# Branch A of an encoder layer: transposes and value products taken for four tiles at a time, blocks turned in place, and a last output piece on another queue

## The chip, the cores and the metric

The kernel runs on one core of one Trainium2 chip. The metric is the device time of one execution in microseconds (us). Engines are named as in the profile: PE is TensorE's matmul side, PEld its weight loads, DVE VectorE, ACT ScalarE, POOL GpSimd, SP SyncE, which here only issues transfers.

## The reference

One encoder layer over two inputs (1024 sample rows, 256 prompt rows; width 1024). Branch A is attention with a window of 128 on either side, 8 query heads on 2 key/value heads, a bias by relative position and a sink logit for each head. Branch B is a dilated attention of three head groups. Both are gated, merged and projected; a squared-ReLU MLP and a last norm follow.

```python
s = jnp.einsum('bnqgrd,bnkgd->bngrqk', qb, kb).astype(jnp.float32) * (dh ** -0.5)
logits = jnp.where(valid[None, :, None, None], s + bias, NEG_INF)
m = jnp.max(logits, axis=-1)
m = jnp.maximum(m, sink_r)                      # branch A only
p = jnp.exp(logits - m[..., None])
denom = jnp.sum(p, axis=-1) + jnp.exp(sink_r - m)
o = jnp.einsum('bngrqk,bnkgd->bnqgrd', p.astype(vb.dtype), vb)
o = o / denom
...
merged = gates[:, :, 0] * (o_a @ w_branch_a) + gates[:, :, 1] * (o_b @ w_branch_b)
x = x + merged @ w_out
return x + jnp.square(jax.nn.relu(rmsnorm(x) @ w_up)) @ w_down     # then a last rmsnorm
```

## The kernel before

The whole program is in stages that PE works through one after the other. Input projections and branch B come first (up to 554 us of the profiled execution), then branch A (554 to 675 us), the gate and branch projections (to 756 us), w_out, and the MLP to the end. Within branch A the order of every engine's instructions is the order in which the code is written (`manual_schedule`).

**Branch A's loop.** There are 1280 rows in ten tiles of 128 (t 0 to 7 sample, 8 and 9 prompt) and four units (u 0 to 3) of two heads each, so 40 steps in `order`; the loop takes two of them per iteration, j = 0, 2, 4, ... A tile sees two or three blocks of 128 keys: blocks for t = 0 to 9 are 2, 3, 3, 3, 3, 3, 3, 2, 2, 2. With two heads a pair of tiles (t even, t+1) has 10, 12, 12, 10 and 8 blocks to turn in the five pairs of a unit.

- `scores(u, t)`: PE multiplies queries and keys into a bank `sc` for each head (L1214, L1215); DVE adds the bias and takes the row maximum in one instruction (L1216) into the tile `s`; a small DVE instruction makes the exponent's bias `nm_a` (L1220).
- `exponential(u, t, h)`: ACT, in place on `s` (L1226), with the row sum.
- `transposes(u, t)`: PE turns every block of a pair into banks of four blocks (L1240), bank tags `pt`, `pt`, `mm`; each bank is copied out to a tile `pt` in SBUF of its own, by ACT, DVE, ACT (`moved`, L282 and L284).
- `values_of(u, t)`: PE multiplies the turned blocks with the values into the one bank `pv` (L1256), with a 128x64 array for each head; DVE copies the result out (L1259), SP stores it to `scr_o`.
- `logits()`, called `fill`: the last gate columns. One `next(fill)` gives PE four matmuls of 512 columns or eight of 256 (L193, bank `mm`, written `mm` in the rows).
- `merge()`, called `merges`: branch B's merge, mostly POOL work with small steps on DVE and ACT in the same in-order queues.

PSUM banks: `bufs={"mm": 3, "sc": 2, "pt": 2, "pv": 1}` (L138), so there are two `pt` banks. In iteration j the code calls `values_of` of pair j-6, `transposes` of pair j-4, `scores` of j, one step of `fill`, the exponentials of j, `scores` of j+1, another step of `fill`, and the exponentials of j+1. At j = 40 `sums_a` closes the row sums, and the load of the sigmoid table and the gates follow. `end` (L1942 and on) makes the last output rows: SP sends both left quarters of the row (L1966), ACT the third quarter and POOL the last one (L1967).

Of the kernel before, what the change touches and what calls it, by code (L numbers as in the profile page):

```python
# [15 lines left out]
P = 128  # L16
# [6 lines left out]
HD = 64  # L23
# [75 lines left out]
def encoder_kernel(  # L99
# [1091 lines left out]
    if True:  # L1191
# [13 lines left out]

        def scores(u, t):
            st, bias = units[u]
            lo, W, c0 = tiles[t]
            s = a3("s", n=4)
            m = small.tile([P, 2], F32, name="m", tag="m")  # L1210
            for h in range(2):
# [5 lines left out]
                    s[:, h, :W], ps[:, :W], bias[:, h, c0 : c0 + W], 1.0, -3.0e38,  # L1217
# [4 lines left out]
            live[u, t] = s  # L1222

        def exponential(u, t, h):
            W, s = tiles[t][1], live[u, t]
            nc.scalar.activation(s[:, h, :W], s[:, h, :W], AF.Exp, bias=nm_a[:, 2 * u + h : 2 * u + h + 1, t],  # L1226
                                 accum_out=l_a[:, 2 * u + h : 2 * u + h + 1, t])

        def transposes(u, t):

            pt = a3("pt", (P, 12, P), 1)
            jobs, at = [], []
            for i in range(2):
                at.append(len(jobs))
                jobs += [(live[u, t + i], b, h) for b in range(tiles[t + i][1] // P) for h in range(2)]
            for i, tag, eng in ((0, "pt", nc.scalar), (4, "pt", nc.vector), (8, "mm", nc.scalar)):
                if i < len(jobs):
                    ps, e = bank(tag, "pt"), min(len(jobs), i + 4)
                    for k, (s, b, h) in enumerate(jobs[i:e]):
                        nc.tensor.transpose(ps[:, P * k : P * k + P], s[:, h, P * b : P * b + P], ident)  # L1240
                    moved(eng, pt[:, i:e, :], ps[:, : P * (e - i)].rearrange("p (i q) -> p i q", q=P))
            for i in range(2):
                live[u, t + i] = pt, at[i]

        def values_of(u, t):

            pv = bank("pv")
            for i in range(2):
                lo, W, _ = tiles[t + i]
                pt, at = live.pop((u, t + i))  # L1250
                v, rest = units[u][0]["v"]
                for b in range(W // P):
                    k = lo + b
                    src = v[:, k, HALVES[u // 2]] if k < 8 else rest[:, k - 8, HALVES[u // 2]]
                    for h in range(2):
# [170 lines left out]
    if True:  # L1426
# [101 lines left out]
        for j in range(0, n + 4, 2):  # L1528
# [629 lines left out]
```

## Time and profile before

| what | value |
|---|---|
| median of three runs | 1660.57 us (1660.44 to 1661.66) |
| the profiled execution | 1661.59 us |
| its span in the trace | 1659.8 us |
| PE busy | 1650.8 us, 99% of the span |
| DVE, ACT, POOL busy | 57%, 43%, 31% |
| granted TensorE clock | 1.00 in every slice |

The page gives each engine's busy time, the span in 40 slices, the DMA queues, the chain that ended last and the costliest groups. In the trace a timeline row reads: start, length, engine, line, operation, output tile <- inputs, shape, count, and in brackets the idle time ahead of it with what ended it. Matmul ends are modelled, so starts are the safer numbers. A piece of the chain reads: start, length, engine, tile and line, count.

### The profile page before, as it was taken

To read this page: it belongs to the slowest core of one execution; us is meant where nothing else is said; L and a number is where in the kernel's file an instruction comes from. 1 tells how busy PE (TensorE), PEld (TensorE's weight loads), DVE (VectorE), ACT (ScalarE), POOL (GpSimd) and SP (SyncE) were. 2 spreads that over 40 slices of the span, in tenths; PEclk is the share of its full clock that TensorE was granted. 3 is DMA by queue.
4 is the path that set the end of the run, shared out by engine and by line. 5 is a ranking of instruction groups with operands and counts; after the bars stand their busy time and mean duration, and the time that the engine had idled before them with its cause. 6 is when DMAs were issued, how large, how long until landed. Compare 5 with 4: busy or idle time off the path is not lost.

```text
span 1659.8 us, 25051 instructions
## 1 busy us (share of the span) xinstructions
PE 1650.8 (99%) x9383; PEld 1404.7 (85%) x9383; DVE 952.5 (57%) x1540; ACT 712.5 (43%) x1478; POOL 516.5 (31%) x397
## 2 busy tenths in 40 slices
PE   9999999999999999999999999999999999999998
PEld 7898888888888888888888888888888888888887
DVE  6732333435555477776478454454456675866665
ACT  6232323325565466653276333333334333333435
POOL 1332222130221525200101555555554250514240
PEclk9999999999999999999999999999999999999999
DMA  7424332655666786955022444344357934733343
GB/s 255 149 70 136 106 110 75 171 145 172 189 201 178 242 245 185 314 192 204 28 87 73 150 148 150 110 145 152 111 172 246 354 119 146 241 102 108 121 121 127
DMA packets 215489, 263.58 MB, mean 159 GB/s; under 512 B 21688, under 2 KB 143816, under 8 KB 215368
## 3 DMA queue, kind: packets, MB, share of 16 engines
q1 hardware_dynamic: 207320, 242.62, 45.8%
q0 software_dynamic: 7712, 18.96, 4.1%
q8 instruction: 74, 1.21, 0.3%
q14 instruction: 47, 0.39, 0.1%
q10 hardware_dynamic: 336, 0.40, 0.1%
HBM read 176.24 MB, written 89.87 MB: 160 GB/s over the span
## 4 chain that ended last, share of the span: by engine, by line
PE 90%; issue 4%; DVE 2%; DMA 2%; ACT 1%; POOL 1%; SPq 0%; POOLq 0%; DVEq 0%; ACTq 0%
PE x L365 20%; PE dn L365 18%; PE mm L193 11%; PE z L365 10%; PE v L863 6%; PE y L365 5%; PE mm L365 5%; PE sc L365 3%; PE pv L365 3%; PE pv L1256 2%; PE pt L1240 2%; PE pt L626 1%; PE sc L590 1%; PE pv L643 1%; PE tr L356 1%
## 5 line engine op out<-in xcount | busy, mean ns | idle before, releaser
L365 PE MATMUL dn<-dhi,ulo 128*128 128x512 f32 x448 | 174.3, 389 | 0.0
L365 PE MATMUL dn<-dlo,uhi 128*128 128x512 f32 x448 | 174.3, 389 | 0.0
L365 PE MATMUL dn<-dhi,uhi 128*128 128x512 f32 x448 | 174.3, 389 | 0.0
L365 PE MATMUL x<-chi,wlo 128*128 128x512 f32 x436 | 171.3, 393 | 0.0
L365 PE MATMUL x<-clo,whi 128*128 128x512 f32 x436 | 170.2, 390 | 0.0
L365 PE MATMUL x<-chi,whi 128*128 128x512 f32 x436 | 169.7, 389 | 0.0
L332 DVE TENSOR_TENSOR wlo<-ta,whi 128x1024 fp32r<-128x1024 f32 x31 | 57.4, 1851 | 183.9 <-ACT whi L330 183.9
L332 DVE TENSOR_TENSOR wlo<-raw,whi 128x1024 fp32r<-128x1024 f32 x62 | 92.8, 1497 | 108.7 <-ACT whi L330 106.1
L411 POOL TENSOR_TENSOR tb<-raw 128x512 f32<-128x512 f32 x26 | 33.9, 1305 | 361.6 <-DMA raw<-in_w_in_dram 122.8
L365 PEld LDWEIGHTS dn<-dhi,ulo 128*128 128x128 f32 x448 | 84.1, 188 | 17.6
L365 PEld LDWEIGHTS dn<-dlo,uhi 128*128 128x128 f32 x448 | 84.1, 188 | 17.3
L365 PEld LDWEIGHTS dn<-dhi,uhi 128*128 128x128 f32 x448 | 84.1, 188 | 17.3
L365 PEld LDWEIGHTS x<-chi,whi 128*128 128x128 f32 x436 | 81.9, 188 | 17.6
L365 PEld LDWEIGHTS x<-chi,wlo 128*128 128x128 f32 x436 | 82.0, 188 | 15.5
L365 PEld LDWEIGHTS x<-clo,whi 128*128 128x128 f32 x436 | 82.1, 188 | 15.0
L1817 POOL TENSOR_TENSOR t<-raw,t 128x1024 f32<-128x1024 f32 x16 | 46.9, 2949 | 149.6 <-DMA raw<-in_w_down_dram 149.5
L187 DVE TENSOR_TENSOR ulo<-uraw,uhi 128x1024 fp32r<-128x1024 f32 x56 | 85.9, 1555 | 5.3 <-ACT uhi L186 5.3
L2001 DVE TENSOR_TENSOR v<-v,dn 128x512 f32<-128x512 f32 x89 | 59.0, 683 | 39.2 <-PE dn L365 39.2
L2101 POOL TENSOR_TENSOR u<-u,u 128x640 f32<-128x640 f32 x16 | 25.1, 1570 | 178.6 <-ACT u L2019 178.6
L187 DVE TENSOR_TENSOR dlo<-raw,dhi 128x1024 fp32r<-128x1024 f32 x32 | 50.3, 1595 | 45.7 <-ACT dhi L186 44.7
L365 PE MATMUL dn<-dhi,up 128*128 128x512 f32 (+1 forms) x232 | 73.9, 382 | 0.0
L365 PE MATMUL z<-chi,wlo 128*128 128x512 f32 x188 | 73.2, 389 | 0.0
(338 smaller groups left out, 4594.1 us busy)
## 6 DMA issues: line engine op xcount, KB each, us to landing
scr_u<-u SPq DMA_DIRECT2D x112, 320.0 KB, 2.5
uraw<-scr_u SPq DMA_DIRECT2D x56, 512.0 KB, 4.4
raw<-in_w_down_dram SPq DMA_DIRECT2D x36, 512.0 KB, 6.5
raw<-in_w_up_dram SPq DMA_DIRECT2D x32, 512.0 KB, 4.8
raw<-in_w_in_dram SPq DMA_DIRECT2D x25, 512.0 KB, 4.9
sg<-scr_g SPq DMA_DIRECT2D x32, 256.0 KB, 6.1
uraw<-scr_u SPq DMA_DIRECT2D x28, 256.0 KB, 4.7
scr_g<-z SPq DMA_DIRECT2D x26, 256.0 KB, 2.9
```

The source lines that it names most:

```text
L187: nc.vector.tensor_tensor(lo, src, hi.bitcast(F32), op=ALU.subtract)
L193: nc.tensor.matmul(ps, a, b, start=i == 0, stop=i == len(seq) - 1)
L332: nc.vector.tensor_tensor(lo, src, hi.bitcast(F32), op=ALU.subtract)
L356: nc.tensor.transpose(ps[:, P * i : P * (i + 1)], xn[t][:, P * k : P * (k + 1)], ident)
L365: nc.tensor.matmul(ps, a, b, start=first and i == 0, stop=last and i == len(seq) - 1, skip_group_check=True)
L411: (nc.vector if vector else nc.gpsimd).tensor_tensor(o, x, y, op=ALU.subtract)
L863: nc.tensor.matmul(ps[:, :n], a, b, start=k == 0 and j == 0, stop=k == KC - 1 and j == 2)
L1240: nc.tensor.transpose(ps[:, P * k : P * k + P], s[:, h, P * b : P * b + P], ident)
L1256: nc.tensor.matmul(pv[HALVES[h], P * i : P * i + P], src, pt[:, at + 2 * b + h, :], start=b == 0, stop=b == W // P - 1, skip_group_check=True)
L1817: nc.gpsimd.tensor_tensor(o, a, b, op=ALU.subtract)
L2001: nc.vector.tensor_tensor(v, v, ps, op=ALU.add)
L2101: nc.gpsimd.tensor_tensor(u[S1], u21, u22, op=ALU.add)
```

## The change

Four tiles (two pairs) are transposed in one run, at iterations with j divisible by 4 (j = 4 to 40), behind the first scores and the first fill step; the value products of two pairs are made in one run at j = 6, 10, ..., 38, and the last ones inside the gate jobs. The blocks of a pair live in one tile `s` of 12 blocks (three such tiles in turn; `pt` in SBUF is gone), with the two heads of a tile in alternate blocks; the turned blocks are copied back to their own places. Banks run `pt`, `pt`, `mm`, `pt`, `pt`, `mm` and the copies alternate ACT and DVE. Two steps of `fill` come ahead of the last transposes. In `end`, SP sends the last quarter in place of POOL.

```diff
+        def blocks_of(u, t):
+            W = tiles[t][1]
+            if t % 2 == 0:
+                live[u, t] = live[u, t + 1] = a3("s", (P, 12, P)), W // HD
+            s, more = live[u, t]
+            return s[:, more : more + W // HD] if t % 2 else s[:, :more]
...
-            s = a3("s", n=4)
+            s = blocks_of(u, t)
...
-                    s[:, h, :W], ps[:, :W], bias[:, h, c0 : c0 + W], 1.0, -3.0e38,
+                    s[:, h::2], ps[:, :W].rearrange("p (b c) -> p b c", c=P),
+                    bias[:, h, c0 : c0 + W].rearrange("p (b c) -> p b c", c=P), 1.0, -3.0e38,
...
-        def transposes(u, t):
...
-            for i, tag, eng in ((0, "pt", nc.scalar), (4, "pt", nc.vector), (8, "mm", nc.scalar)):
...
+        def transposes(pairs):
+            k = 0
+            for u, t in pairs:
+                s, n = live[u, t][0], (tiles[t][1] + tiles[t + 1][1]) // HD
+                for i in range(0, n, 4):
+                    e = min(n, i + 4)
+                    ps = bank(("pt", "pt", "mm")[k % 3], "pt")
+                    for x in range(i, e):
+                        nc.tensor.transpose(ps[:, P * (x - i) : P * (x - i) + P], s[:, x], ident)
+                    moved((nc.scalar, nc.vector)[k % 2], s[:, i:e], ps[:, : P * (e - i)].rearrange("p (i q) -> p i q", q=P))
+                    k += 1
...
-            if j > 4:
-                values_of(*order[j - 6])
-            if j > 2:
-                transposes(*order[j - 4])
+            if j % 4 == 2 and 5 < j < n:
+                values_of((order[j - 6], order[j - 4]))
             if j == n:
                 sums_a()
+                steps_of(fill, 2)
             if j < n:
                 scores(*order[j])
                 next(fill)
-                for h in range(2):
-                    exponential(*order[j], h)
+                if j % 4:
+                    exponentials(*order[j])
+            if j % 4 == 0 and j:
+                transposes((order[j - 4], order[j - 2]))
+            if j < n:
+                if j % 4 == 0:
+                    exponentials(*order[j])
                 scores(*order[j + 1])
...
-                steps_of(fill, 2)
                 for i in range(2):
                     open_gate(i)
...
-        side = {1: [(lambda last: values_of(*last), order[n - 2])], 2: [(high_b, 1)], 3: [(low_b, 1)],
+        side = {1: [(values_of, (order[n - 4], order[n - 2]))], 2: [(high_b, 1)], 3: [(low_b, 1)],
...
-                (nc.scalar if q.start else nc.gpsimd).dma_start(y_rows(row)[:, 512 + q.start : 512 + q.stop], b[:, q])
+                (nc.scalar if q.start else nc.sync).dma_start(y_rows(row)[:, 512 + q.start : 512 + q.stop], b[:, q])
```

**PE at j = 12, before.** A matmul of 64x128 here is a value product, `pt<-ident,s` a transposed block, `sc` a score; names in brackets are the engines whose semaphores it waits for.

```order
L1256 MATMUL pv<-pt,va 64x128 [waits Activation_49]
L1256 MATMUL pv<-pt,va 64x128 x7
L1256 MATMUL pv<-pt,va 64x128 [waits Activation_49]
L1256 MATMUL pv<-pt,va 64x128
L1240 MATMUL pt<-ident,s 128x128 [waits PE_49]
L1240 MATMUL pt<-ident,s 128x128 x3
L1240 MATMUL pt<-ident,s 128x128 [waits PE_49]
L1240 MATMUL pt<-ident,s 128x128 x3
L1214 MATMUL sc<-kk,q 128x384 [waits DVE_49]
```

Values, transposes and scores follow one another in every iteration.

**PE at j = 12, in the changed program:** the run of transposes of two pairs (here 8 and 10 blocks), behind a fill matmul and ahead of scores.

```order
L193 MATMUL mm<-hhi,whi 128x512
L1250 MATMUL pt<-ident,s 128x128 [waits Activation_49] x2
L1250 MATMUL pt<-ident,s 128x128 x2
L1250 MATMUL pt<-ident,s 128x128 [waits Activation_49] x2
L1250 MATMUL pt<-ident,s 128x128 x2
L1250 MATMUL pt<-ident,s 128x128 [waits Activation_49] x2
L1250 MATMUL pt<-ident,s 128x128 x2
L1250 MATMUL pt<-ident,s 128x128 [waits Activation_49]
L1250 MATMUL pt<-ident,s 128x128 x3
L1250 MATMUL pt<-ident,s 128x128 [waits DVE_49]
L1250 MATMUL pt<-ident,s 128x128
L1222 MATMUL sc<-kk,q 128x384
```

The run is five banks long; the fourth starts with a wait for ACT and the fifth with one for DVE.

**PE at j = 10, in the changed program:** the run of value products of two pairs, between a fill matmul and scores.

```order
L193 MATMUL mm<-hhi,whi 128x512
L1267 MATMUL pv<-s,va 64x128 x8
L1267 MATMUL pv<-s,va 64x128 [waits Activation_49]
L1267 MATMUL pv<-s,va 64x128 x3
L1267 MATMUL pv<-s,va 64x128 [waits DVE_49]
L1267 MATMUL pv<-s,va 64x128 x3
L1267 MATMUL pv<-s,va 64x128 [waits Activation_49]
L1267 MATMUL pv<-s,va 64x128 x3
L1267 MATMUL pv<-s,va 64x128 [waits DVE_49]
L1267 MATMUL pv<-s,va 64x128
L1222 MATMUL sc<-kk,q 128x256 [waits DMAHW1_49,DVE_49]
```

Behind the values there are scores now, where there were transposes.

**ACT at the end of branch A (j = 38 and 40), before:** `whi` is the high part of a branch weight, `nm_a` the sink's exponential, `gs` a gate column.

```order
L244 ACTIVATE whi<-raw 128x1024 [waits DMAHW2_49,DMAHW3_49,DMAHW1_49,DMAHW7_49,DMAHW0_49,Pool_49]
L282 ACTIVATE pt<-pt 128x512 [waits PE_49,Activation_49]
L282 ACTIVATE pt<-pt 128x256 [waits PE_49]
L1469 ACTIVATE nm_a<-nm_a 128x80 [waits DVE_49]
L1273 ACTIVATE gs<-mm 128x512 [waits DMAHW3_49,DMAHW2_49,DMAHW5_49,DMAHW1_49,Pool_49]
L1516 ACT_TABLE_LOAD
```

**ACT at the same place in the changed program.**

```order
L244 ACTIVATE whi<-raw 128x1024 [waits DMAHW3_49,DMAHW2_49,DMAHW4_49,DMAHW0_49,Pool_49]
L1482 ACTIVATE nm_a<-nm_a 128x80 [waits DVE_49]
L1286 ACTIVATE gs<-mm 128x512 [waits DMAHW5_49,DMAHW6_49,DMAHW1_49,DMAHW7_49,PE_49,Pool_49]
L282 ACTIVATE s<-pt 128x512 [waits PE_49]
L282 ACTIVATE s<-pt 128x256 [waits PE_49]
L282 ACTIVATE s<-pt 128x512 [waits PE_49]
```

The copies out of the banks have moved behind the sink's exponential and the gate column's copy.

## Rows read from the trace of the kernel before

**Rows 1.** Page: engines' busy time, and granted clock in 40 slices.

```profile
PE 1650.8 (99%) x9383; PEld 1404.7 (85%) x9383; DVE 952.5 (57%) x1540; ACT 712.5 (43%) x1478; POOL 516.5 (31%) x397
...
PEclk9999999999999999999999999999999999999999
```

**Rows 2.** Stretches: span, busy of PE, PEld, DVE, ACT, POOL, clock, DMA, GB/s.

```profile
562.00:674.00 112.00, 112.00 (x969) 97.29 (x969) 77.51 (x246) 77.20 (x209) 56.53 (x60) 1.00 0.78 223
675.00:700.00 25.00, 25.00 (x133) 21.55 (x132) 19.70 (x35) 14.32 (x29) 6.17 (x10) 1.00 1.06 283
```

**Rows 3.** Chain that ended last, branch A: start, length, work.

```profile
562.88 1.09 PE pt L1240 x10
...
584.52 1.24 PE pv L1256 x20
585.76 1.02 PE pt L1240 x8
...
600.52 0.93 PE mm L193 x4
601.45 1.46 PE pv L1256 x24
602.91 1.46 PE pt L1240 x12
```

**Rows 4.** Timeline of PE where values are followed by a 512-column matmul.

```profile
673.28 1.10 PE L1256 MATMUL pv<-pt,vp 128*64 128x128 f32 x16
674.30 0.50 PE L193 MATMUL mm<-obhi,wlo 128*128 128x512 f32 x1
674.64 0.39 PE L193 MATMUL mm<-oblo,whi 128*128 128x512 f32 x1
674.87 0.40 PE L193 MATMUL mm<-obhi,whi 128*128 128x512 f32 x1
```

**Rows 5.** Timeline, one run of 12 transposes and its three copies.

```profile
625.26 1.53 PE L1240 MATMUL pt<-ident,s 128*128 128x128 f32 x12
...
626.02 0.60 ACT L282 ACTIVATE pt<-pt 128x512 f32<-128x512 f32 x1 [0.58 <-PE pt L1240]
...
626.47 0.69 DVE L284 COPY pt<-pt 128x512 f32<-128x512 f32 x1 [0.66 <-PE pt L1240]
...
626.83 0.60 ACT L282 ACTIVATE pt<-pt 128x512 f32<-128x512 f32 x1 [0.21 <-PE pt L1240]
```

**Rows 6.** Timelines of PE and ACT: a tile's last score, its last exponential.

```profile
622.83 0.33 PE L1215 MATMUL sc<-kk,q 128*128 128x384 f32 x1
...
624.75 0.60 ACT L1226 ACTIVATE s<-s,nm_a 128x384 f32<-128x384 f32 x1
```

**Rows 7.** The same at another tile, and `nm_a` over all 40.

```profile
583.26 0.33 PE L1215 MATMUL sc<-kk,q 128*128 128x384 f32 x1
...
585.90 0.17 DVE L1328 COPY cb<-cb 128x16 f32<-128x16 f32 x1 [1.03 <-DMA cb<-scr_n]
...
587.57 0.61 ACT L1226 ACTIVATE s<-s,nm_a 128x384 f32<-128x384 f32 x1
...
L1220 DVE SCALAR_TENSOR_TENSOR nm_a<-m,nsink x40: 161/163/1447, 557.7 to 663.5; 128x2 f32<-128x2 f32 x40
```

**Rows 8.** Timeline of PE and ACT at the end of branch A.

```profile
662.63 0.28 PE L1215 MATMUL sc<-kp,qp 128*128 128x256 f32 x1
...
664.72 1.04 ACT L244 ACTIVATE whi<-raw 128x1024 fp32r<-128x1024 f32 x1
...
667.48 0.59 ACT L1273 ACTIVATE gs<-mm 128x512 f32<-128x512 f32 x1
```

**Rows 9.** PE's waits in the gate stage, 674 to 760 us.

```profile
PEld mm L193 <- DVE sg L1615: 0.4, 1, 0.4
```

**Rows 10.** Last transfers: timeline, then queue issues to landing, 1630 to 1665 us.

```profile
1655.50 0.59 POOL L1967 DMA_DIRECT2D out_dram<-v  x1 [51.68 <-ACT v L1965]
1655.57 0.38 SPq L1966 DMA_DIRECT2D out_dram<-v  x1
...
out_dram<-v SPq DMA_DIRECT2D x2, 128.0 KB, 1.8
out_dram<-v POOLq DMA_DIRECT2D x1, 128.0 KB, 2.6
```

More of the change, by code (lines that the diff above doesn't have):

```diff
@@ L1245, in values_of, with exponentials @@
-        def values_of(u, t):
+            ready_s[u, t] = s
+        ready_s = {}
+        def exponentials(u, t):
+            s = ready_s.pop((u, t))
+            for h in range(2):
+                nc.scalar.activation(s[:, h::2], s[:, h::2], AF.Exp, bias=nm_a[:, 2 * u + h : 2 * u + h + 1, t],
+                                     accum_out=l_a[:, 2 * u + h : 2 * u + h + 1, t])
+        def transposes(pairs):
[9 more added lines that the diff above has]
+                    k += 1
@@ L1247, in values_of @@
+        def values_of(pairs):
             pv = bank("pv")
-            for i in range(2):
-                lo, W, _ = tiles[t + i]
-                pt, at = live.pop((u, t + i))
+            for x, (u, t) in enumerate(pairs):
                 v, rest = units[u][0]["v"]
-                for b in range(W // P):
-                    k = lo + b
-                    src = v[:, k, HALVES[u // 2]] if k < 8 else rest[:, k - 8, HALVES[u // 2]]
-                    for h in range(2):
-                        nc.tensor.matmul(pv[HALVES[h], P * i : P * i + P], src, pt[:, at + 2 * b + h, :],
-                                         start=b == 0, stop=b == W // P - 1, skip_group_check=True)
@@ L1258, in values_of @@
-            o = qslot("o", (P, 2, P))
-            nc.vector.tensor_copy(o, pv[:, : 2 * P].rearrange("p (i q) -> p i q", i=2))
-            nc.sync.dma_start(scr_o[t // 2][:, u], o)
+                for i in range(2):
+                    lo, W, _ = tiles[t + i]
+                    pt, more = live.pop((u, t + i))
+                    at = more if i else 0
+                    for b in range(W // P):
+                        k = lo + b
+                        src = v[:, k, HALVES[u // 2]] if k < 8 else rest[:, k - 8, HALVES[u // 2]]
+                        for h in range(2):
+                            nc.tensor.matmul(pv[HALVES[h], 2 * P * x + P * i : 2 * P * x + P * i + P], src,
+                                             pt[:, at + 2 * b + h, :],
+                                             start=b == 0, stop=b == W // P - 1, skip_group_check=True)
@@ L1262, in logits @@
+            for x, (u, t) in enumerate(pairs):
+                o = qslot("o", (P, 2, P))
+                nc.vector.tensor_copy(o, pv[:, 2 * P * x : 2 * P * x + 2 * P].rearrange("p (i q) -> p i q", i=2))
+                nc.sync.dma_start(scr_o[t // 2][:, u], o)
         def logits():
@@ L1548, in encoder_kernel @@
                     steps_of(merges, 1 + j // 2 % 2)
-                for h in range(2):
-                    exponential(*order[j + 1], h)
+                exponentials(*order[j + 1])
             if j == n - 4:
```

18 lines of the change are left out of this document (removed).

## The prediction

> **What bounds the kernel now.** I read the page first. PE is busy for 99% of the span at a granted clock of 1.00 in all slices [rows 1], so only what PE itself does, or is made to wait for, moves the time; DVE's 57% and ACT's 43% matter only where PE comes to wait for them. Then the stretches: in branch A, 562 to 674 us, PE is busy for all 112.0 us, with DVE and ACT at 77 us each [rows 2]. So a gain in branch A must come from PE, and there is room for new waits, since each of the two that empty the banks is two thirds full. Then the chain, which in branch A is PE piece after PE piece: there the lengths of runs of different counts give pitch and fixed cost [rows 3]. Last come timelines for how long an emptied bank takes, when the exponentials end, and the end of the kernel [rows 5 to 8, 10]. The profiled execution took 1661.59 us with a span of 1659.8; the median is 1660.57. The terms below are differences, so I add them to the median; on the profiled execution they would be added to 1661.59.
>
> **Part 1, fewer changes of run: -2.55 us.** Runs of values take 1.46 us for 24 and 1.24 for 20, so 0.055 a matmul, and 1.46 - 24 x 0.055 leaves 0.15 fixed. Runs of transposes take 1.46 for 12 and 1.02 for 8, so 0.11 a block and again 0.15 fixed. But the one run that follows fill matmuls takes 1.09 for 10, so nothing fixed [rows 3]. The 0.15 is thus paid on entering values from full-array work and on leaving them. What leaving costs into a 512-column matmul is seen once: 16 values from 673.28 are over at about 674.20 (0.05 + 8 x 0.109), the next starts at 674.30, and its successor 0.34 behind it where 0.23 is the pitch: 0.10 + 0.11 = 0.20 [rows 4]. Before, there are 20 entries, 19 exits into transposes and one into a matmul: 20 x 0.15 + 19 x 0.15 + 0.20 = 6.05 us. After, there are 10 entries, and 10 exits, 9 of them into scores, for which the trace has no row: between the 0.15 into transposes and the 0.20 into a matmul. Scores are matmuls like the latter, so 0.20. The transposes now follow fill matmuls: nothing. That is 1.5 + 2.0 = 3.5, a gain of 2.55 (up to 3.05 with 0.15). The matmuls themselves stay the same in number. The copies are one to one too, except that for two pairs DVE has up to three where it had two, and ACT three where it had four; nobody waits for that by itself, since values come two scores and a fill step later.
>
> **Part 2, two `pt` banks for runs twice as long: +2.0 us.** Before, a run uses three different banks and never waits for one. Now the fourth bank is the first one again, and the fifth the second. In a run of 12 the first copy starts 0.76 us behind the first transpose, 0.71 without the entry from values, and takes 0.60 on ACT; DVE's takes 0.69 [rows 5]. So the first bank is free 1.31 us after the run's start. PE is there after 12 blocks, 12 x 0.109 = 1.31, or, at the four places that begin with a pair of 10 blocks (j = 4, 20, 24, 40), after 1.09. The second bank is free at 0.44 + 0.71 + 0.69 = 1.84, and PE wants it at 16 x 0.109 = 1.74. So six places lose 0.10, four about 0.31 (0.22 and 0.09): 1.85 us. A restart may expose up to a fixed part of 0.15 in each [rows 3]: 3.5 at most. On the other side the third copy of the run in the rows started 0.32 behind its last transpose where the first took about 0.38; with that the loss is 1.3. I take 2.0, nearer to the lower end, since that copy too is one that a free engine started.
>
> The Trainium skill speaks against the change here: TensorEngine Tiling (Array Packing), PSUM Bottleneck, says that packing the array speeds TensorE up but not the emptying of PSUM, so that the copy may become the bound, and that both ScalarE and VectorE should be used for it. The changed kernel does use both, and the copies' rate (0.69 for two banks of 0.87) would hold; by the rule as a bound of each run the sum would be the slow rival's below, by the rows it is 2.0 us.
>
> **Part 3, exponentials that come closer to their transposes: +0.7 us.** Before, an iteration lies between a pair's exponentials and its transposes; now only two fill steps and one tile's scores lie between the later pair's last exponentials and the run, and ACT's copies are queued behind them. A last score at 622.83 had its exponential done at 625.35, 2.52 us later [rows 6]. The run starts 0.17 + 0.92 + 0.70 + 0.92 = 2.71 behind that score (a score, fill, scores of 384 columns, fill), and ACT's first copy is due at 3.42: 0.9 us to spare. Where that isn't enough: at j = 12 the exponential ended 4.92 us behind the score, since DVE stood until 585.90 at a merge step for a DMA [rows 7]; PE now arrives with one more pair's values done (1.1 us), so about 0.4 late. At j = 40 ACT has the branch weight (done at 665.76), `nm_a` and the gate column's 0.59 ahead of the copies [rows 8]: 4.0 behind the score, where the run starts after three fill steps and the first copy is due at 3.6: 0.4. And `nm_a` takes 0.16 as a rule, but up to 1.45 [rows 7], with which three or four more places are 0.1 to 0.5 late. All of it would be 1.9, none of it 0; I take 0.7, the two named places nearly whole. The two fill steps moved ahead of the last transposes are cover (1.8 us of PE), not new work.
>
> **Part 4, the end: -0.4 us.** POOL's piece is issued at 1655.50 and lands 2.6 later, at 1658.1; SP is free at about 1656.0, and its small pieces take 1.8: 1657.8 [rows 10]. That is 0.3 less; the landing times alone differ by 0.8, and if the third piece on SP takes as long as POOL's it is 0.5 worse. I take 0.4.
>
> **The gate stage: 0.** There the DMA share is 1.06 [rows 2] and PE's weight loads wait for DVE once, 0.4 us [rows 9]. SP's stores and gate loads keep their order but for the last `scr_o` stores; what PE gains ahead of that stage could be lost at this wait, so 0 to +0.4.
>
> **The sum:** -2.55 + 2.0 + 0.7 - 0.4 = -0.25: 1660.3 us. A measurement of this kernel can tell about 0.2%, 3.3 us, from no change; so I forecast no change.
>
> **The rivals.**
> - *The banks keep up.* If copies start as soon as the data are there and no exponential is late, parts 2 and 3 are at most 0.5: -2.55 + 0.5 - 0.4 = 1658.1, and 1656.7 with the best of every bound (-3.05 - 0.8). For it: both copy engines have a third of their time idle [rows 2]. Against: the 0.10 of the second bank comes from lengths that don't change.
> - *Slower: ACT's queue becomes the bound of the runs.* Each run's first copy stands behind the exponentials of the tile before, and these behind DVE's `nm_a`. If the 1.3 us by which `nm_a` can be late [rows 7] falls on it at half the ten places and pushes past the 0.9 to spare, and banks are at their upper end: 3.5 + 1.9 + 5 x 0.4 - 2.55 - 0.4 = +4.4, 1665.0. The waits of the runs must pass 2.95 us for slower at all, 6.2 for over 0.2%. For it: DVE and ACT share that queue with the merge; against: the median of `nm_a` is 0.16.
> - *The changes of run are not saved.* If the 0.15 is the price of any start of transposes or values, the longer program has as many as before but one kind: 10 x (0.15 + 0.20 + 0.15) = 5.0, a gain of 1.05, and the sum 1661.8. Against it stands the piece of 1.09 [rows 3].
> - *The clock.* If a run of 24 transposes counted as idle time, TensorE would fall from 2.4 to 1.2 GHz and each of the 208 blocks take another 0.109: +22.7, some 1683. In the trace the runs of 12 stand behind runs of values at the granted clock 1.00 [rows 1, 2]. By a rule of the Trainium skill (TensorE: Matmul & The Clock Gate, Part 4: PE-mode transpose) transposes don't count as PE work for the clock; no row here shows a fall.
>
> **How the numbers follow.** Chances: the forecast 0.62 (1658.9 to 1662.0), the banks keep up 0.18, slower 0.13, not saved 0.05, the clock 0.02. Faster by over 0.2% needs 1657.25 or less: a quarter of the second, 0.05. Slower by over 0.2% (1663.9 or more): half of the third and the clock, 0.09. The rest is 0.86. The range 1657.6 to 1662.8 holds the forecast, most of the second and the start of the third.
>
> **What would show it.** Right: runs of transposes behind fill with no fixed part; values with 0.15 + 0.20; gaps on PE of 0.1 to 0.4 at the fourth and fifth bank, with ACT and DVE as their releasers (PE's waits in 560 to 675 us, none now, would be 2 to 3 us); the copies starting 0.7 behind; SP's piece as the last to land. Wrong: no wait of PE in those runs (then 1658), waits above 1 us for ACT (then slower), or a change elsewhere than in 554 to 675 us and the last 3 us.

## The result, and the profile after

The changed kernel takes 1665.53 us (median of 8 runs, 1664.78 to 1667.65) where the kernel before, beside it, takes 1661.28 (8 runs, 1660.44 to 1664.47). The ratio is 1.0026, 95% interval 1.0015 to 1.0037: it is slower by some 4.25 us, clear of no change and past the line of 0.2% that the prediction drew. The forecast was 1660.3 and no change, in a range that ended at 1662.8. In a second group of 11 runs it took 1665.53 again, ratio 1.0021 (1.0012 to 1.0030). Of all runs told of here one is slow, e4_pairs' at 5855.78 us, and the numbers below leave it out.

The page still shows a PE that is busy nearly always, beside [rows 1], and the shares of the chain are much as before (PE 90%, issue 4%, DVE 2%, DMA 2%, ACT 1%), so neither says where the time went.

```profile
PE 1651.9 (99%) x9383; PEld 1405.2 (84%) x9383; DVE 953.4 (57%) x1546; ACT 708.7 (43%) x1472; POOL 513.8 (31%) x396
...
PE 93%; DMA 3%; DVE 2%; ACT 2%; issue 0%; SPq 0%; ACTq 0%; DVEq 0%
```

**Where the time went, by stages.** All traces have the same 9383 matmuls on PE (e5_gate 20 fewer), so the start of the same-numbered matmul can be set beside that of the kernel before. I count branch A from the 3585th matmul (553.93 us before) to the 4591st (673.99, one of the last values), the gate stage to the 4829th (718.13), and the end from the last matmul to the span's end. Up to branch A no trace differs by more than 0.3 us (but for e12_fill, 1.8), and between gate stage and last matmul all take 934.64 to 934.71 us.

| profiled execution | its time | branch A | gate stage | end |
|---|---|---|---|---|
| before | 1661.59 | 120.06 | 44.14 | 7.02 |
| after | 1667.65 | 125.55 | 45.38 | 6.34 |
| after, a second time (e8_again) | 1664.17 | 123.98 | 43.49 | 6.34 |

The profiled execution of after lies 2.1 us above its median. The second one, 1.4 below, says which part of that is scatter: the gate stage (45.38 and 43.49), and a wait ahead of branch A's first fill matmul, 1.3 us in the first, none in the second, and 0.4 in the kernel before. What stays is branch A, 3.9 us longer than before in the second profile, and the end, 0.68 shorter.

**Where in branch A.** PE's waits from 554 to 766 us, line by line: who waited, for whom, us in sum, times, longest. Before there were only two here, of 0.2 each.

```profile
PE pt L1250 <- DVE s L284: 2.4, 4, 0.9
PE mm L193 <- ACT z L1067: 1.0, 1, 1.0
PE mm L193 <- DVE mT L1628: 0.8, 1, 0.8
PE sc L1222 <- DVE m L1224: 0.7, 2, 0.5
PE pt L1250 <- ACT s L282: 0.2, 1, 0.2
```

The list counts an idle time only from the modelled end of the matmul ahead. By starts (beyond the usual 0.109) the first blocks of late banks lose, at j = 4, 8, 12, ... 40: 0.26, 0.31 + 0.79, 0.36, 0, 0.26, 0.26, 0.60, 0, 0.60 + 1.02, 0.26: 4.7 us in sum, and 4.8 in the second profile at the same places to 0.04. The block behind such a one, and the first two of other banks from the fourth on, are 0.03 to 0.06 late as well. With these the runs of transposes lose 5.8 us (5.9 in the second profile): 0.42, 1.21, 0.41, 0.13, 0.35, 0.35, 0.63, 0.20, 1.70 and 0.43. Before, they lost 1.1 in all: the second block of each of the 19 runs behind values came 0.06 late. Scores (`sc` for DVE) lose 1.2, in the second profile 0.8.

The worst run is the one at j = 36. Timelines of PE, DVE and ACT, columns as ahead of the prediction:

```profile
659.36 1.47 PE L1250 MATMUL pt<-ident,s 128*128 128x128 f32 x12
661.27 0.63 PE L1250 MATMUL pt<-ident,s 128*128 128x128 f32 x4 [0.44 <-DVE s L284]
662.75 1.09 PE L1250 MATMUL pt<-ident,s 128*128 128x128 f32 x8 [0.85 <-DVE s L284]
...
660.43 0.69 DVE L284 COPY s<-pt 128x512 f32<-128x512 f32 x1 [0.92 <-PE pt L1250]
662.00 0.69 DVE L284 COPY s<-pt 128x512 f32<-128x512 f32 x1 [0.88 <-PE pt L1250]
...
659.58 1.04 ACT L244 ACTIVATE whi<-raw 128x1024 fp32r<-128x1024 f32 x1
660.53 1.06 ACT L282 ACTIVATE s<-pt 128x512 f32<-128x512 f32 x2
```

The fourth bank starts at 661.27, 0.15 after DVE's copy of the second bank ended (661.12), and the fifth at 662.75, 0.06 after DVE's copy of the fourth (662.69). ACT's copy of the first bank was over by 661.1 and nobody took that bank: the pool (the program's allocator of banks) gave one and the same bank for the second, the fourth and the fifth. It can be read without any trace, from PE's order. At j = 24 the run is (from its fourth bank on)

```
L1250 MATMUL pt<-ident,s 128x128 [waits Activation_49]
L1250 MATMUL pt<-ident,s 128x128 x3
L1250 MATMUL pt<-ident,s 128x128 [waits DVE_49]
```

as at j = 12, which stands ahead of the prediction; at j = 28 the fourth bank waits for DVE:

```
L1250 MATMUL pt<-ident,s 128x128 [waits DVE_49,Activation_49]
L1250 MATMUL pt<-ident,s 128x128 [waits Activation_49]
L1250 MATMUL pt<-ident,s 128x128 x2
L1250 MATMUL pt<-ident,s 128x128 [waits Activation_49]
```

The longest wait of scores, at 622.08, and what DVE did ahead of it:

```profile
622.08 0.45 PE L1222 MATMUL sc<-kk,q 128*128 128x384 f32 x1 [0.48 <-DVE m L1224]
...
618.21 0.76 DVE L1272 COPY o<-pv 128x256 f32<-128x256 f32 x2 [2.19 <-PE pv L1267]
...
619.95 0.47 DVE L1229 SCALAR_TENSOR_TENSOR nm_a<-m,nsink 128x2 f32<-128x2 f32 x1
620.34 1.21 DVE L236 TENSOR_TENSOR wlo<-raw,whi 128x1024 fp32r<-128x1024 f32 x1
621.47 0.55 DVE L1224 CUSTOM_DVE_ANT_0 s<-sc,bias 128x384 f32<-128x384 f32 x1
```

The reduction that frees the score bank starts at 621.47, behind two copies of values, a slow `nm_a` and a weight's low part. At the end, the three pieces on SP and the one on ACT (us from issue to landing), beside [rows 10]:

```profile
out_dram<-v SPq DMA_DIRECT2D x3, 128.0 KB, 1.9
out_dram<-v ACTq DMA_DIRECT2D x1, 128.0 KB, 2.2
```

### The profile page after: what moved, and what is told of

It reads as the page before. It is cut to its first block, busy times and chain, and to the rows that moved or that the text cites. A ratio compares the mean times of both kernels' runs of the same rounds, so it can differ in the third digit from the quotient of the medians.

```text
span 1665.9 us, 25062 instructions
## 1 busy us (share of the span) xinstructions
PE 1651.9 (99%) x9383; PEld 1405.2 (84%) x9383; DVE 953.4 (57%) x1546; ACT 708.7 (43%) x1472; POOL 513.8 (31%) x396
## 3 DMA queue, kind: packets, MB, share of 16 engines
q1 hardware_dynamic: 207464, 242.75, 45.7%
q8 instruction: 74, 1.21, 0.3%
## 4 chain that ended last, share of the span: by engine, by line
PE 93%; DMA 3%; DVE 2%; ACT 2%; issue 0%; SPq 0%; ACTq 0%; DVEq 0%
PE dn L365 23%; PE x L365 20%; PE mm L193 10%; PE z L365 10%; PE v L863 6%; PE y L365 5%; PE mm L365 5%; PE sc L365 3%; PE pv L365 3%; DMA sg<-scr_g 1%; PE pv L1267 1%; PE pt L626 1%; PE sc L590 1%; PE pt L1250 1%; PE pv L643 1%; DMA scr_g<-gs 1%
## 5 line engine op out<-in xcount | busy, mean ns | idle before, releaser
L365 PEld LDWEIGHTS dn<-dhi,uhi 128*128 128x128 f32 x448 | 84.1, 188 | 17.5
L365 PEld LDWEIGHTS dn<-dlo,uhi 128*128 128x128 f32 x448 | 84.1, 188 | 17.5
L365 PEld LDWEIGHTS x<-chi,whi 128*128 128x128 f32 x436 | 81.9, 188 | 17.5
L187 DVE TENSOR_TENSOR dlo<-raw,dhi 128x1024 fp32r<-128x1024 f32 x32 | 50.1, 1589 | 45.2 <-ACT dhi L186 44.3
```

The costliest lines, as they stand in the source:

```text
L187: nc.vector.tensor_tensor(lo, src, hi.bitcast(F32), op=ALU.subtract)
L365: nc.tensor.matmul(ps, a, b, start=first and i == 0, stop=last and i == len(seq) - 1, skip_group_check=True)
```

## The experiments

The stages of each profiled execution, as above, and the times of each group's runs against the kernel before in the same group:

| kernel | median us | ratio to before (95%) | branch A | gate stage | end |
|---|---|---|---|---|---|
| e1_turn | 1664.09 | 1.0009 (0.9999, 1.0019) | 122.97 | 45.04 | 6.34 |
| e2_olater | 1670.54 | 1.0046 (1.0034, 1.0059) | 128.59 | 45.66 | 6.35 |
| e3_tail | 1661.72 | 0.9995 (0.9986, 1.0004) | 123.52 | 44.52 | 6.34 |
| e4_pairs | 1662.63 | 1.0000 (0.9991, 1.0009) | 118.63 | 50.21 | 6.34 |
| e5_gate | 1660.46 | 0.9991 (0.9983, 1.0000) | 118.01 | 43.79 | 7.03 |
| e6_pool | 1664.38 | 1.0013 (1.0003, 1.0022) | 124.12 | 43.49 | 6.35 |
| e7_pairs_end | 1661.13 | 0.9994 (0.9985, 1.0003) | 119.73 | 44.33 | 6.33 |
| e8_again | 1665.53 | 1.0021 (1.0012, 1.0030) | 123.98 | 43.49 | 6.34 |
| e9_best | 1659.70 | 0.9985 (0.9975, 0.9995) | 118.52 | 45.57 | 6.35 |
| e10_early | 1664.68 | 1.0015 (1.0007, 1.0024) | 121.03 | 46.72 | 6.34 |
| e11_end | 1663.32 | 1.0004 (0.9995, 1.0012) | 123.17 | 43.77 | 6.33 |
| e12_fill | 1660.20 | 0.9993 (0.9983, 1.0002) | 118.35 | 43.78 | 6.35 |

The kernel before had medians of 1662.41 (e1 to e4), 1661.37 (e5 to e8), 1661.76 (e9, e10) and 1662.32 (e11, e12) beside them.

**e1_turn: banks by turn.**

```diff
     def bank(tag, name=None):
+        if tag == "pt":
+            pt_turn[0] ^= 1
+            return psum.tile([P, 512], F32, name=name or tag, tag="pt%d" % pt_turn[0], bufs=1)
...
```

> The changed kernel, with one edit: the two pt banks are given out strictly by turn. In the changed kernel the pool gives the fourth bank of the runs at j = 28 and j = 36 the bank that DVE empties second, and the fifth at j = 36 the same bank once more; its trace shows PE waiting there 0.60, 0.60 and 1.02 us. Theory 'choice of bank': by turn these three waits fall to about 0.26 or less each, as at j = 4, 20, 24 and 40, and the time by 1.5 to 2.0 us, to about 1663.8. Rival 'late copies': the copies at those places are late because ACT and DVE have other work queued ahead of them (a weight's high part of 1.04 us at j = 36); then PE waits for ACT's copy instead, the sum of the waits in runs stays at 4 to 4.7 us and the time at 1665.5.

Measured 1664.09, near the 1663.8 of the choice of bank; the intervals of the two ratios overlap, so it is the trace that settles it. In the timeline of PE the run at j = 36 no longer shows a break (the view begins behind the first of its 24 blocks):

```profile
657.75 2.95 PE L1255 MATMUL pt<-ident,s 128*128 128x128 f32 x23
```

and of PE's waits for scores and banks in 554 to 766 us this is left:

```profile
PE sc L1227 <- DVE m L1229: 1.3, 1, 1.3
PE pt L1255 <- ACT s L287: 1.2, 3, 0.8
PE pt L1255 <- DVE s L289: 0.6, 1, 0.6
```

By starts the first blocks at j = 28 and 36 lose 0.33 us where they lost 2.22. But those at j = 20 and 40 grew from 0.26 to 0.42 and 0.92, so the first blocks lose 3.6 us in sum, not 2.8, and the wait for scores shown above grew from 0.64 to 1.45. The choice of bank is thus shown for 1.9 of the 4.7 us; the 1.1 at j = 8 did not move.

**e2_olater: value results copied behind the scores' reductions.**

```diff
-                values_of((order[j - 6], order[j - 4]))
+                out = values_of((order[j - 6], order[j - 4]))
...
                 scores(*order[j])
+                if j % 4 == 2 and j > 5:
+                    values_out(*out)
                 next(fill)
```

> The changed kernel, with one edit: the two copies of value results (0.76 us on DVE, one after the other) and their stores come behind the next tile's scores instead of ahead of them, so that DVE reduces those scores first. The trace of the changed kernel shows PE waiting for DVE at the second tile of scores behind a run of values, 0.64, 0.36 and 0.20 us. Theory 'two copies ahead of the reductions': these 1.2 us go, and the time falls to about 1664.3. Rival 'DVE is late for another reason' (a small exponent-bias instruction that takes up to 1.25 us instead of 0.16, or a weight's low part of 1.21 us in its queue): the waits stay at 0.6 us or more, and the time is 1665 to 1666.

Measured 1670.54, 5 us slower than the changed kernel: the theory fell, and in the other direction. The timeline of DVE at the place of the wait shown above, with the edit:

```profile
618.79 0.56 DVE L1224 CUSTOM_DVE_ANT_0 s<-sc,bias 128x384 f32<-128x384 f32 x1 [2.82 <-PE sc L1223]
...
619.95 0.75 DVE L1276 COPY o<-pv 128x256 f32<-128x256 f32 x2
```

PE's waits in branch A:

```profile
PE pt L1250 <- DVE s L284: 3.2, 5, 0.9
PE sc L1222 <- DVE m L1224: 2.5, 4, 0.8
PE pt L1250 <- ACT s L282: 1.0, 3, 0.4
```

The first reduction starts 0.76 us behind its score (618.03) with the copies out of its way, and 0.79 (618.88 behind 618.09) with them ahead: there the copies lie in time in which DVE waits for the score anyway, and cost nothing. Moved behind, they stand ahead of the weight's low part and the next tile's reductions, and PE's wait at this place grew from 0.64 us to 0.98. The waits for scores went from 1.2 us to 3.4 by starts, those in the transposes from 4.7 to 6.1; among them one more wait of 1.02 us for a bank given twice in a row, at j = 28, since the pool's choice changed with the order.

**e3_tail: the end alone.**

```diff
-                (nc.scalar if q.start else nc.gpsimd).dma_start(y_rows(row)[:, 512 + q.start : 512 + q.stop], b[:, q])
+                (nc.scalar if q.start else nc.sync).dma_start(y_rows(row)[:, 512 + q.start : 512 + q.stop], b[:, q])
```

> The kernel before, with only the last part of the change: SyncE instead of GpSimd sends the last quarter row. From the two traces, PE's last matmul is 6.74 us later and the end 6.06 us later, so this part should be worth -0.7 us: 1660.6 where the kernel before takes 1661.3. Rival: the 0.7 is scatter of the last transfer's landing, and the time stays within 0.2 us of the kernel before.

The ratio says -0.8 us, with an interval from -2.3 to +0.7; the trace says it to a hundredth: 7.02 us from the last matmul to the end before, 6.33 to 6.35 in every kernel with the edit, 7.03 in e5_gate without it. Branch A of this profile is 3.5 us longer although its code is that of the kernel before; it is told of in the last section.

**e4_pairs and e7_pairs_end: transposes one pair at a time.** Both keep the values of two pairs in one run. e4_pairs:

```diff
+            if j % 4 == 0 and j:
+                transposes((order[j - 4],))
             if j == n:
                 sums_a()
                 steps_of(fill, 2)
...
-            if j % 4 == 0 and j:
-                transposes((order[j - 4], order[j - 2]))
+            if j == n:
+                transposes((order[j - 2],))
...
                 scores(*order[j + 1])
+                if j % 4 == 0 and j:
+                    transposes((order[j - 2],))
```

> The changed kernel, but the transposes are made for one pair (at most three banks) at a time: the earlier pair's at the start of the iteration, the later pair's behind the second tile of scores; value products stay in runs of two pairs. Theory 'a run of five or six banks on two pt banks is what costs': PE waits nowhere in the transposes (4.7 us in the changed kernel), the change of run costs -2.3 us against the kernel before (-1.5 in the changed kernel, and 0.08 less at each of ten more ends of transposes), and the end -0.7; with 0 to 1.3 for waits of scores and 0 to 1.2 in the gate stage the time is 1658.3 to 1660.8, below the kernel before. Rival 'copies and exponentials are late whatever the length of the run' (ACT and DVE queues): waits of 2 to 4 us remain in the transposes or move to the values, and the time is 1663 or more.

PE waits nowhere in the transposes, so their waits come from runs longer than the banks; branch A takes 1.4 us less than before, in spite of one wait of 1.0 for scores at j = 8. But the gate stage took 50.2 us, part of it at the lower clock (last section). PE's waits there:

```profile
PE mm L193 <- DVE mT L1632: 3.6, 4, 1.3
```

and what the chain says of them, two of its pieces in 676 to 712 us:

```profile
684.65 0.32 SPq L1524
...
685.03 17.54 DMA sg<-scr_g
```

A gate column's load took 17.5 us from 685.03 to its landing. e7_pairs_end puts the end of branch A back into the old order:

```diff
             if j == n:
                 sums_a()
-                steps_of(fill, 2)
-            if j == n:
-                transposes((order[j - 2],))
+            if j == n + 2:
+                transposes((order[j - 4],))
...
                 steps_of(merges, 2)
+                steps_of(fill, 2)
                 for i in range(2):
                     open_gate(i)
```

> As e4_pairs (one pair's transposes at a time, values of two pairs in one run), but with the end of branch A in the order of the kernel before: the last two fill steps behind the last row sums' closing and the last pair's transposes one iteration later. In e4_pairs branch A took 1.4 us less than in the kernel before and the gate stage behind it 6.1 more. Theory 'the order at the end of branch A makes the gate stage late': the stage loses 0 to 0.5 us and the time is about 1659.3. Rival 'the gate stage is bound by its loads': whatever branch A gains is taken back there, and the time stays at 1661 to 1662.

The gate stage took 44.3 us, and the time is 0.2 us below the kernel before beside it, where e4_pairs was 0.2 above (medians; the intervals of the two ratios overlap). The median time from issue to landing of the half-size gate loads in 676 to 700 us, in e4_pairs:

```profile
sg<-scr_g SPq DMA_DIRECT2D x8, 128.0 KB, 14.5
```

and in e7_pairs_end:

```profile
sg<-scr_g SPq DMA_DIRECT2D x9, 128.0 KB, 9.4
```

The time did not reach the 1659.3 of the theory, since two waits remain in branch A (1.04 for scores at j = 8; 0.70 for the bank of the row sums).

**e5_gate: PE earlier at the gate stage.**

```diff
+                if u < 3:
+                    nc.tensor.matmul(ps[:, :W], q, st["k"][1][:, P * lo : P * lo + W], start=True, stop=False)
-                nc.tensor.matmul(ps[:, :W], q, st["k"][0][:, P * lo : P * lo + W], start=False, stop=True)
+                nc.tensor.matmul(ps[:, :W], q, st["k"][0][:, P * lo : P * lo + W], start=u == 3, stop=True)
```

> The kernel before, with the first of the two products of a score left out in the last unit (20 matmuls of 0.11 to 0.17 us fewer; that unit's scores lack their low part). PE reaches the gate stage about 3 us earlier, with everything else as it was. Theory 'the gate stage is bound by its loads': its end stays where it was (the stage from the last values on takes 44.1 us in the kernel before; it would take 46 to 47), and the time falls by less than 1 us. Rival 'PE bounds the gate stage': the 3 us are there at the end, 1658.3 where the kernel before takes 1661.3.

Branch A took 2.05 us less and the gate stage 43.79 us, not 46: the loads do not bound that stage by themselves. The runs scatter (1659.28 to 1661.06, but for one), and their ratio, 0.9991, holds 1.5 of the 2.05 us.

**e6_pool: GpSimd's part of the merge cut.**

```diff
-                        nc.gpsimd.tensor_tensor(m, m, c, op=ALU.add)
+                        nc.gpsimd.tensor_tensor(m[:, :8], m[:, :8], c[:, :8], op=ALU.add)
```

(and the multiplication ahead of it in the same way)

> The changed kernel, with GpSimd's multiplications and additions of branch B's second and third part cut to a small piece (most of that merge is left out; the first part's multiplications are whole). In both traces every small exponent-bias instruction on DVE that takes over 0.25 us (11 of 40 in the changed kernel, 6.7 us more than 0.16 each) ends within 0.05 us of the end of a GpSimd tensor instruction. Theory 'GpSimd holds DVE up, and that makes PE wait for scores and banks': with GpSimd nearly idle the excess falls below 2 us, the waits for scores (1.2 us) to 0.6 or less, and the waits in the transposes by 0.5 to 1; the time by 1 to 2 us. Rival 'DVE's own queue': the small instructions get short, but PE's waits stay within 0.5 us of what they were, since copies and weights' low parts stand in the same queue.

`nm_a` no longer takes long (0.8 us over 0.16 each in sum, against 6.7), but PE's waits in the transposes are what they were:

```profile
PE pt L1250 <- DVE s L284: 2.4, 4, 0.9
PE mm L193 <- ACT z L1067: 0.5, 1, 0.5
PE sc L1222 <- DVE m L1224: 0.3, 1, 0.3
PE pt L1250 <- ACT s L282: 0.2, 1, 0.2
```

By starts they are 4.7 us again. Of the waits for scores 0.47 is left, the one behind the weight's low part. So GpSimd makes 0.3 to 0.7 us of the waits for scores and nothing of those for banks: for the banks the rival, DVE's own queue, held, and for the scores the theory. The median, 1664.38, is 1.15 us below that of e8_again in the same group, as the theory had it; but these waits explain only 0.3 to 0.7 of that, and no profile shows the rest.

**e8_again: the changed kernel once more.** No edit.

> The changed kernel once more, beside the others of this group. Theory 'the waits are fixed by the order of the program': the waits in the transposes (4.7 us), for scores (1.2) and in the gate stage (1.2) are the same ones at the same places, to 0.3 us in sum. Rival 'they are scatter': other places or other lengths. The 0.9 us ahead of branch A's first matmul, where PE waited for a copy behind a transfer, should be gone if it was scatter, and stay if the change caused it.

The waits in the transposes are the same to 0.04 us at each place: they are fixed by the order. Those for scores (0.8 against 1.2) and the gate stage are not, and the 0.9 us ahead of branch A's first fill matmul is gone.

**e10_early and e11_end: the weight's halves, and the end.** e10_early is e1_turn with the first gate weight's halves a fill step earlier:

```diff
+                    for x, _ in enumerate(mm3(...)):
+                        yield
+                        if i == 0 and t0 == NS and x == 1:
+                            prepare()
...
-                    if i + 1 < len(PLAIN) and t0 == NS:
+                    if 0 < i < len(PLAIN) - 1 and t0 == NS:
                         prepare()
```

> As e1_turn (the changed kernel with banks by turn), with the first gate weight's halves made one fill step earlier. At j = 8 PE waited 0.30 and 0.79 us in e1_turn's run of transposes, for copies that stood behind these halves (1.05 us on ACT, 1.23 on DVE). Theory 'the weight's halves in the copies' queues': the two waits fall to about 0.3 together, and the time by 0.8, to about 1663.3. Rival 'two banks for a run of six are too few there by themselves': they stay at 0.8 to 1.1 us, and the time at 1664.1.

The two waits at j = 8 went altogether (one of 0.40 for scores took their place), which is 0.7 us; branch A fell to 121.0 us, 1.9 less than in e1_turn, since other waits were shorter as well. The time did not fall: the gate stage took 46.7. e11_end has the last two runs and fill steps in the old order:

```diff
             if j == n:
+                transposes((order[j - 4],))
                 sums_a()
-                steps_of(fill, 2)
...
-            if j % 4 == 0 and j:
+            if j % 4 == 0 and 0 < j < n:
                 transposes((order[j - 4], order[j - 2]))
+            if j == n + 2:
+                transposes((order[j - 4],))
...
                 steps_of(merges, 2)
+                steps_of(fill, 2)
```

> As e10_early, but the end of branch A in the order of the kernel before: the last four tiles are turned as two runs of one pair, an iteration apart, and the last two fill steps come behind the closing of the row sums. In e10_early branch A took 121.0 us (120.1 in the kernel before), but the gate stage 46.7 (44.1), and the time stayed at 1664.7. Theory 'the changed order at the end of branch A makes the gate stage late once branch A is short': the gate stage takes 43.5 to 44.5 us and the time falls by 2 to 2.5 us, to about 1662.4. Rival 'the gate stage is bound by its loads, whatever the order': it takes 46 or more again, and the time stays at 1664 to 1665.

The gate stage took 43.8 us, as the theory wants; branch A grew by 2.1 (0.9 at the end for the row sums, the rest mostly in longer waits at j = 20 and 36 and for scores), and the ratio fell from 1.0015 to 1.0004, 1.8 us where the theory wanted 2 to 2.5. The half-size gate loads land, in 676 to 700 us, in e10_early after

```profile
sg<-scr_g SPq DMA_DIRECT2D x8, 128.0 KB, 14.2
```

and in e11_end after

```profile
sg<-scr_g SPq DMA_DIRECT2D x8, 128.0 KB, 10.4
```

**e9_best and e12_fill: the two waits that were left.** e9_best is e7_pairs_end with the weight's halves early and

```diff
             if j == n + 2:
-                transposes((order[j - 4],))
+                later = transposes((order[j - 4],), True)
...
                 rows_a()
+                for x in later:
+                    moved(*x)
```

> As e7_pairs_end, with two edits against the two waits of PE left in its branch A: the first gate weight's halves (1.04 us on ACT, 1.22 on DVE) are made one fill step earlier, so that they no longer stand ahead of the copies and reductions at j = 8 (PE waited 1.04 us for scores there); and the copies of the last pair's turned blocks come behind the copy of the row sums (PE waited 0.70 us for that bank). Theory 'what stands in DVE's and ACT's queues ahead of a bank's copy is what PE waits for': both waits go, branch A takes 118.0 to 118.4 us (119.7 in e7_pairs_end, 120.1 in the kernel before), and the time is 1659.3 to 1659.8, where the kernel before takes 1661.3. Rival: the waits move to the next scores or to the values and the time stays at 1661.

1659.70 us, ratio 0.9985 (0.9975 to 0.9995): below the kernel before by some 2 to 2.5 us, clear of no change by its interval though within the prediction's 0.2%, and below the changed one by some 6. Branch A took 118.5, one wait of 0.8 us having come up for the row sums' reciprocals. e12_fill puts fill steps there:

```diff
             if j == n + 2:
+                run(fill)
                 rows_a()
```

> As e9_best, with the rest of the fill steps ahead of the row sums' transpose instead of behind it: PE waited 0.83 us there for DVE's reciprocals, and has 0.9 us of fill to do. Theory: the wait goes, branch A takes 117.7 us and the time is about 1658.9. Rival: the 0.8 us comes back in the gate stage (45.6 us in e9_best's profile), and the time is the same as e9_best's, 1659.7.

The wait moved by one matmul (0.87 us for the bank of the row sums) and the time is not below e9_best's (ratio 0.9993 against 0.9985). Nor did the rival's 0.8 us come back in the gate stage, which took 43.8 in this profile.

## Why the prediction was wrong, point by point

The forecast was a sum of -2.55 + 2.0 + 0.7 - 0.4 + 0. What the traces give in its place is about -2.5, then +5.9 (for 2.0 + 0.7), then +1.0 for scores (forecast at nothing), then -0.7, and -0.65 to +1.24 for the gate stage. Branch A's 3.9 us in the second profile are the first three, less the 0.4 us for which PE waited ahead of its first fill matmul before, and not there. The step that failed is the price of the banks in a long run, Part 2 above all: it took the two `pt` banks to come by turn and each copy to start as soon as its data were there.

**Part 1 (-2.55) came out at -2.5, in part by luck.** The changes of run behave as forecast: transposes behind fill start at the usual pitch (10 gaps of 0.20 on average), values into scores cost 0.15 and 0.05 more at the score's second half. Summed by the kind of neighbours in branch A (second profile of after against before), the gaps between starts change by -3.86 (values to transposes, 19 gone), -1.10 (the late second blocks behind values), -3.03 (into values, 20 to 10), +1.82 (values to scores), +1.75 (fill to transposes), -0.25 (transposes to scores, 18 to 9), +1.61 (20 more gaps inside longer runs) and +0.58 (within scores): -2.5. The luck is in two terms that the forecast did not have and that pull against each other. One is the -1.10. The other comes from the chain, whose ends are modelled: "Runs of transposes take 1.46 for 12" [rows 3], but by starts the same run takes 1.28, in the timeline of PE before:

```profile
602.84 1.53 PE L1240 MATMUL pt<-ident,s 128*128 128x128 f32 x12
604.12 0.36 PE L1214 MATMUL sc<-kp,qp 128*128 128x256 f32 x1
```

which is 12 x 0.109 less 0.03: a score starts 0.08 sooner behind a transposed block than another block would. That gain goes with the number of runs, and the change halved it, +0.7 us.

**Part 2 (+2.0) failed at two steps.** The first is the sentence "Now the fourth bank is the first one again, and the fifth the second." Where it holds and nothing else is queued, the price was about right: 0.35 to 0.43 us at j = 4, 20, 24 and 40 where 0.31 was forecast, 0.13 and 0.20 at j = 16 and 32 where 0.10 was. At j = 28 and 36 the pool chose otherwise, which cost 2.33 us where 0.20 was forecast; e1_turn shows it, and the order of the changed program had it all along. The second is the first copy 0.71 us behind the run's start, taken from one run [rows 5] in which both engines were free. At j = 8 a weight's halves stood ahead of both engines' copies, and DVE's first copy started 2.15 us behind the run's start (579.04 and 576.89): 1.21 us where 0.10 was forecast, and 0.13 in e10_early, which takes the halves away. (The upper end, 3.5, is 3.35 by its own terms, 1.85 + 10 x 0.15; nothing hangs on it.)

The prediction weighed the rule of the Trainium skill (TensorEngine Tiling (Array Packing), PSUM Bottleneck) that the copy out of PSUM may become the bound. The trace agrees for these runs, not for the stage: in 562 to 674 us DVE and ACT are no busier than before (75.9 and 68.5 us, where [rows 2] has 77.5 and 77.2), and in e4_pairs, with the same copies in shorter runs, every block of a run starts 0.109 behind the last, with no wait.

**Part 3 (+0.7)** was right at j = 12 (0.41 in all for 0.4 and the 0.10 of Part 2): the exponentials ended 0.94 us behind the run's start there, and ACT's first copy began behind them. It was wrong at j = 40, where ACT's first copy began 0.72 behind the run's start. In e1_turn, with PE earlier at that place, the same queue did make it late: 1.36 behind, and PE lost 0.92.

**The waits for scores (0.8 to 1.2) were missing.** "The copies are one to one too ... nobody waits for that by itself" looked at who uses the copied values, not at what stands behind in DVE's queue: the reductions that free the score banks. Ahead of them stand weights' low parts of 1.2 us, `nm_a` held up by GpSimd, and two copies. e6_pool shows 0.3 to 0.7 us for `nm_a`; the low part's share is read from the timeline and was not tested apart in the changed kernel (from e7_pairs_end to e9_best, in another order, a wait for scores of 1.04 us at j = 8 went with the weight's halves made earlier). That the copies alone make it was my first theory here, and e2_olater overthrew it.

**Part 4 (-0.4)** was right in kind and too small: -0.67 to -0.69 in each of the twelve profiles with the edit. Its own rows gave -0.3.

**The gate stage (0 to +0.4)** was wrong in its range. The seven profiles with the changed order at the end of branch A (after, e1, e2, e4, e6, e8, e10) took 43.5 to 50.2 us, 45.7 on average; the seven with the old order (before, e3, e5, e7, e9, e11, e12) 43.8 to 45.6, 44.3 on average. The median landings of the half-size gate loads in 676 to 700 us are 9.7 to 14.5 us in the first seven and 8.0 to 10.4 in the others. With e4 against e7 and e10 against e11, that points to the order. But there is one profile of each kernel, the same program (after and e8_again) gave 13.6 and 10.3 us for the loads and 45.4 and 43.5 for the stage, and without e4's 50.2 the first average is 45.0. So how much of the 1.4 us is the order and how much the scatter of landings stays open.

**The rivals.** "ACT's queue becomes the bound of the runs" gave 1665.0, close to what came, but its mechanism (late `nm_a` and exponentials) did not come, except at j = 12: e6_pool made `nm_a` short and the waits for banks stayed. The number is luck. "Changes of run not saved" and "the clock" did not come: with runs of up to 24 transposes no stretch of branch A fell below a granted clock of 1.00 in the changed kernel. The chance of slower, 0.09, was too low: the six places priced at 0.10 us each came from one run [rows 5] and one place of the order, and three of them (j = 8, 28 and 36) cost 3.5 us together.

## What to carry over

Where a pool hands out banks, read from the order which bank each run gets, at every place and not at one; a bank that is handed out twice in a row costs a whole copy. Count what else stands in the copying engines' queues at each place, and read the lengths of runs from starts, not from modelled ends, with the small gaps at every restart: they made 1.1 us on either side here. Group what has no bank to wait for (here the values of two pairs), and leave runs that need banks no longer than the banks.

## What the runs showed of the hardware

**DVE and GpSimd.** In the changed kernel each of the 11 small `nm_a` instructions that took over 0.25 us ended within 0.05 us of the end of a GpSimd instruction, as here (632.84 + 1.25 = 634.09; 632.51 + 1.56 = 634.07):

```profile
632.84 1.25 DVE L1229 SCALAR_TENSOR_TENSOR nm_a<-m,nsink 128x2 f32<-128x2 f32 x1
...
632.51 1.56 POOL L1413 TENSOR_TENSOR r<-r 128x512 f32<-128x512 f32 x1
```

With GpSimd's work cut (e6_pool) their excess fell from 6.7 us to 0.8. The Trainium skill (SBUF — State Buffer, SBUF: two separate sides) says that a DVE instruction with two inputs from SBUF and a GpSimd instruction that reads SBUF hold a shared pair of ports one at a time, each for its whole length; the trace agrees.

**The clock behind a wait.** In e3_tail's profile DVE stood at a step of the merge for a transfer (2.73 us and 0.69), PE then waited 2.3 us for a score bank, and the granted clock fell from 1.00 to 0.50 (2.4 to 1.2 GHz). PE's row:

```profile
590.33 0.57 PE L1214 MATMUL sc<-kk,q 128*128 128x384 f32 x1 [2.27 <-DVE m L1216]
```

and stretches of two us (busy times of PE, PEld, DVE, ACT, POOL, then clock, DMA share, GB/s):

```profile
588.00:590.00 2.00, 0.06 (x1) 0.00 (x0) 1.89 (x7) 1.10 (x4) 0.00 (x0) 1.00 1.04 214
590.00:592.00 2.00, 1.67 (x5) 1.57 (x6) 1.58 (x8) 1.90 (x6) 0.00 (x0) 0.62 1.10 213
592.00:594.00 2.00, 2.00 (x10) 1.17 (x10) 1.83 (x8) 2.00 (x7) 0.00 (x0) 0.52 0.99 288
594.00:596.00 2.00, 2.00 (x25) 1.83 (x22) 0.60 (x3) 0.55 (x1) 0.77 (x1) 1.00 1.04 369
```

512-column matmuls start 0.43 us apart there where 0.23 is usual, so this wait cost 2.4 us and some 1.4 more. In e4_pairs the same came behind two waits of 1.5 and 1.4 us in the gate stage. The single waits of 1.0 us (after, j = 36) and of 1.45 us (e1_turn, for scores) had no such effect: the granted clock stayed at 1.00. The late transfer in e3_tail thus cost that run some 3.8 us in a stage that the edit does not touch, which is the size of the scatter between runs here.
